# Seven products instead of eight for ten row tiles of an output projection, with four of the seven gathered in one PSUM bank

## The chip, the cores and the metric

The kernel runs on one core of one Trainium2 chip. The metric is the device time of one execution in microseconds; every operand is fp32. Matrix products in full precision are made of three passes: each operand is split into a high part and the rest (a low part), and high x high, high x low and low x high are summed in PSUM. So a product over 128 rows, 512 columns and a depth of 128 is three matmuls, here called one chunk.

The engines are TensorE (PE; PEld is its weight load), VectorE (DVE), ScalarE (ACT), GpSimd (POOL) and SyncE (SP), which issues nearly all DMAs. ACT, DVE, POOL, SP and PE all run their instructions in the order in which the program writes them (`manual_schedule`); a wait at the head of one of them holds up all that stands behind it there.

## The reference

An encoder layer of two halves, for 256 prompt and 2048 sample rows (2304 together, T in the code, 18 tiles of 128 rows):

```python
q, k, v, z_a, u_f, z_f = jnp.split(rms_norm(x, g_pre) @ w_in, ...)
y_a = neighbourhood_attention(q, k, v, rpb)
y_f = fourier_mix(u_f, w_fourier, b_fourier)
mixed = concatenate([rms_norm(y_a, g_na) * silu(z_a),
                     rms_norm(y_f, g_f) * silu(z_f)], -1)
return x + rms_norm(mixed @ w_out, g_post)
```

`mixed @ w_out` has a depth of 1024: 512 of the attention half, 512 of the Fourier half, and 1024 output columns. The row scale of each half's norm is applied to the half's product, as it comes out of PSUM; g_na and g_f are folded into the weights.

## The kernel before

The program first makes all projections and the Fourier half (to about 598 us). Then comes the attention phase: 36 groups G[k], k = 0 to 35 (4 pairs of heads, pr, times 9 blocks of queries, i), one per step of the loop at L1642, and at last 18 tiles of the attention half's output product (L1804).

A step k does on PE, in this order: `scores` of group k (into four PSUM banks: three of tag `a`, which has three, one of tag `b`, which has two); the first transposes of group k-1 (`transp`, into the two banks `ptb`); half of an output product of the Fourier half (`f_mm`, 6 matmuls, L1497); the second transposes of k-1; the other half (6 matmuls); `pv` of k-1 (into the one bank of tag `c`). The Fourier half's output product is here to fill PE: step k makes output half n = k % 2 of row tile k // 2, a depth of four chunks, into one bank of tag `b` (`po`). `f_evac` takes it out with the row scale `invf`: DVE for n = 0 (L1529), ACT for n = 1 (L1526), which also stores the 128 x 1024 row tile to `oD`.

On the other engines in a step: `bias_max` (four on DVE, L1251) and `exps` (four on ACT) of group k; `soft`, two calls of two scalings each, on POOL (L1263); the copies of the transposes (h = 0 on ACT, L1572, h = 1 on DVE, L1574); `split_q` of group k+1 (qh on ACT, ql on POOL, L1209); every second step `ys_split` of the next row tile (yh on ACT, L1483, yl on DVE, L1488) and `ys_mul` (the product with silu(z) on POOL, L1474); in steps with i = 5 to 8 `split_k` for the next pair of heads (kh on ACT, L1140, kl on POOL, L1141); then y (DVE, L1600) and its square (ACT L1606, POOL L1607) from `pv`. `norm_sums` and `norm_turn` make the row scales at the steps of the table NT.

Tiles come from pools with a fixed number of buffers; a new tile of a tag waits until the oldest one of that tag has been read for the last time. `gt` takes from a pool of 13 buffers of 4 KB a partition (output tiles `ofs`, the Fourier weights `wo1`: eight tiles `wo1[n][c]` of output half n and chunk c, high and low part).

Of the kernel before, what the change touches and what calls it, by code (L numbers as in the profile page):

```python
# [10 lines left out]
F32 = mybir.dt.float32  # L11
F32R = mybir.dt.float32r
AF = mybir.ActivationFunctionType
ALU = mybir.AluOpType
# [160 lines left out]
def build(tc, A, O):  # L175
# [1262 lines left out]
    gpb = sm.tile([128, D], F32, name="gpb", bufs=1)  # L1438
# [24 lines left out]
    def ys_load(d):  # L1463
# [4 lines left out]
        if half:  # L1468
            d["z"] = sm.tile([128, 4, 128], F32, tag="yz", name="yz", bufs=1)
            nc.sync.dma_start(d["z"], zD[0, :, ts].rearrange("(c p) t -> p c t", p=128))  # L1470
# [5 lines left out]
    def y_parts(d):  # L1476
        d["h"] = sm.tile([128, 4, 128], F32R, tag="yh", name="yh", bufs=3)
        d["l"] = sm.tile([128, 4, 128], F32R, tag="yl", name="yl")
# [6 lines left out]
    def y_lo(d):  # L1485
        if "l" not in d:
            d["l"] = sm.tile([128, 4, 128], F32R, tag="yl", name="yl")
        V.tensor_tensor(out=d["l"], in0=d["raw"], in1=d["h"].bitcast(F32), op=ALU.subtract)  # L1488
# [14 lines left out]
    def xt_load(d):  # L1503
        d["xt"] = gt([128, D], F32, "xt")
        nc.sync.dma_start(d["xt"], A["xn"][d["t"] * 128:d["t"] * 128 + 128, :])
# [7 lines left out]
    def a_mm(d, n, js=range(12)):  # L1513
        if js[0] == 0:
            d["p", n] = ps.tile([128, 512], F32, tag="a" if n else "b", name="po", bufs=3 if n else 2)
        out_mm(d, n, js, d["p", n], lambda n, x, c: WO[x][:, c, n * 512:n * 512 + 512])
# [62 lines left out]
    def pv(g):  # L1579
# [28 lines left out]
        if R is None or hc:  # L1608
            nc.sync.dma_start(yD[0, pr, :, ts], y)

    WO = []

    WK = (24, 26, 28, 29, 31, 32, 33, 34)
    NT = {4: range(2, 4), 8: range(4, 8), 10: range(8, 12), 11: range(12, 16), 12: range(16, 18),
          32: range(4), 34: range(4, 8), 36: range(8, 12)}

# [25 lines left out]
    for k in range(2, len(G) + 1):  # L1642
# [13 lines left out]
        if k == 9:  # L1656
            nc.sync.dma_start(gpb, pbc(A["gpost"]))
        if k == 23:
            wp = pt.enter_context(tc.tile_pool(name="wp", bufs=1, side="right"))
            WO.extend(wp.tile([128, 4, D], F32R, name="w0%d" % x) for x in range(2))  # L1660
        if k in WK:
            y = WK.index(k)
            nc.sync.dma_start(WO[y % 2][:, y // 2].bitcast(F32), woD[y % 2, y // 2])
        x = k // 2 + 1
        if g:
            scores(g)
            if 2 < k < 34 and k % 2 == 0:
                ys_mul(ftiles[x])
                if x + 1 < 18:
                    ys_load(ftiles[x + 1])  # L1670
            bias_max(g, 0, 0)
            exps(g, 0, 0)
            bias_max(g, 0, 1)
            bias_max(g, 1, 0)
# [3 lines left out]
        if g:  # L1678
            exps(g, 0, 1)
            bias_max(g, 1, 1)  # L1680
            exps(g, 1, 0)
            f_mm(k, range(6))
# [21 lines left out]
        if g:  # L1704
            f_mm(k, range(6, 12))
        else:
            a_mm(atiles[0], 1, range(6))
        if k % 2 and x < 18:
# [5 lines left out]
        if g:  # L1714
            f_evac(k)
# [6 lines left out]
        if k == 12:  # L1722
            pq_.close()
        if k + 1 < len(G):
            prep_v(G[k + 1])
        if k + 3 < len(G):
            prep(G[k + 3])
        if k == 28:
            xk = [kp.tile([128, T], F32, tag=x, name="xk") for x in ("kh", "kl")]
        if 32 <= k < 36:  # L1730
            x, d = k - 32, atiles[k - 32]
            d["xt"] = xk[x // 2][:, x % 2 * D:x % 2 * D + D]
            nc.sync.dma_start(d["xt"], A["xn"][d["t"] * 128:d["t"] * 128 + 128, :])
        if k == 32:
            ys_load(atiles[0])
        if k in (34, 35):
            ys_load(atiles[k - 33])
            of_load(atiles[k - 34])


    def evac(d, p, ns, q):
# [3 lines left out]
        jk = sm.tile([128, 512], F32, tag="jk", name="jk", bufs=1)  # L1745
# [36 lines left out]
    def last_tile(d, b):  # L1782
        og = d["og"] = gt([128, D], F32, "og")
        nc.gpsimd.tensor_tensor(out=og[:, :512], in0=d["of"][:, :512], in1=gpb[:, :512], op=ALU.mult)
        for q, ns in enumerate((slice(512, 896), slice(896, 1024))):
            p = ps.tile([128, 384], F32, tag="a", name="pl", bufs=3)[:, :ns.stop - ns.start]
            for j in range(12):
                c, x = divmod(j, 3)
                nc.tensor.matmul(p, (d["l"] if x == 2 else d["h"])[:, c], WO[x == 1][:, c, ns], start=j == 0,
                                 stop=j == 11)  # L1790
# [13 lines left out]
    for j, d in enumerate(atiles):  # L1804
        if j + 3 < 18:
            ys_load(atiles[j + 3])
        for x in range(2, 5) if j == 0 else (j + 4,):
            if x < 18:
                of_load(atiles[x])
                if x > 3:  # L1810
                    xt_load(atiles[x])
# [40 lines left out]
```

## Time and profile before

| | |
|---|---|
| median of 3 runs | 958.79 us (958.73 to 958.92) |
| span of the profiled execution | 957.4 us (its own time is not listed) |
| mean granted TensorE clock | 0.997 |
| PE busy | 949.5 us, 5625 matmuls |
| DVE, ACT, POOL busy | 707.8, 494.8, 435.4 us |
| attention phase with the Fourier half's product | about 598 to 847 us |
| steps k = 12, 13, 14, 15, 16 begin | 677.3, 684.7, 692.2, 699.7, 707.1 us |

A row of a timeline reads: start, duration (us), engine, line, operation, output <- inputs, shapes, how many; in brackets the idle time of the engine just before and what ended it. A row of a source line reads: how many, and the shortest, median and longest duration in ns. A row by stretch reads: the stretch, its length, then busy time and count of PE, PEld, DVE, ACT, POOL, then the granted clock, the DMA share and GB/s. Durations of neighbours on DVE and ACT overlap by some 0.07 us.

### The profile page before, as it was taken

To read this page: it belongs to the slowest core of one execution; us is meant where nothing else is said; L and a number is where in the kernel's file an instruction comes from. 1 tells how busy PE (TensorE), PEld (TensorE's weight loads), DVE (VectorE), ACT (ScalarE), POOL (GpSimd) and SP (SyncE) were. 2 spreads that over 40 slices of the span, in tenths; PEclk is the share of its full clock that TensorE was granted. 3 is DMA by queue.
4 is the path that set the end of the run, shared out by engine and by line. 5 is a ranking of instruction groups with operands and counts; after the bars stand their busy time and mean duration, and the time that the engine had idled before them with its cause. 6 is when DMAs were issued, how large, how long until landed. Compare 5 with 4: busy or idle time off the path is not lost.

```text
span 957.4 us, 16751 instructions
## 1 busy us (share of the span) xinstructions
PE 949.5 (99%) x5625; PEld 790.3 (83%) x5625; DVE 707.8 (74%) x1298; ACT 494.8 (52%) x1068; POOL 435.4 (45%) x411
## 2 busy tenths in 40 slices
PE   9999999999999999999999999999999999999997
PEld 8889988888888888888888779788788888888886
DVE  6758987787975865697887369776666656659997
ACT  6735676423334532233344267677676766644443
POOL 4100002465750302575566055567678686524444
PEclk9999999999999999999999999999999999999998
DMA  9899697557758894499889997788877998989993
GB/s 357 297 383 334 245 343 264 187 193 280 296 190 331 304 342 144 175 345 356 306 297 340 335 329 247 232 241 271 262 241 239 285 301 255 287 289 346 330 346 129
DMA packets 140077, 269.80 MB, mean 282 GB/s; under 512 B 13178, under 2 KB 80464, under 8 KB 136728
## 3 DMA queue, kind: packets, MB, share of 16 engines
q1 hardware_dynamic: 139640, 268.32, 80.5%
q8 instruction: 45, 0.74, 0.3%
q10 hardware_dynamic: 288, 0.40, 0.1%
q14 instruction: 40, 0.33, 0.1%
q0 software_dynamic: 64, 0.02, 0.0%
HBM read 179.00 MB, written 96.81 MB: 288 GB/s over the span
## 4 chain that ended last, share of the span: by engine, by line
PE 98%; DVE 1%; DMA 0%; issue 0%; DVEq 0%
PE po L1497 20%; PE mm L166 18%; PE mm L164 18%; PE mm L165 18%; PE pv L1586 6%; PE ptb L1570 6%; PE s L1229 4%; PE py L164 1%; PE py L165 1%; PE py L166 1%; PE ptb L1043 1%; DMA x<-x 0%; PE pab L1053 0%; PE ppq L1096 0%; PE pz L166 0%; PE pz L164 0%
## 5 line engine op out<-in xcount | busy, mean ns | idle before, releaser
L164 PE MATMUL mm<-xh,wa 128*128 128x512 f32 x448 | 174.4, 389 | 0.0
L165 PE MATMUL mm<-xl,wa 128*128 128x512 f32 x448 | 174.3, 389 | 0.0
L166 PE MATMUL mm<-xh,wa 128*128 128x512 f32 x448 | 174.3, 389 | 0.0
L545 POOL TENSOR_TENSOR ws<-wr 128x512 f32<-128x512 f32 x16 | 23.4, 1465 | 217.8 <-DVE wa L560 127.6
L1263 POOL TENSOR_SCALAR w<-w,m 128x465 f32<-128x465 f32 (+9 forms) x136 | 84.8, 635 | 46.2 <-DVE m L1260 35.5
L166 PEld LDWEIGHTS mm<-xh,wa 128*128 128x128 f32 x448 | 84.1, 188 | 17.6
L164 PEld LDWEIGHTS mm<-xh,wa 128*128 128x128 f32 x448 | 84.1, 188 | 17.5
L165 PEld LDWEIGHTS mm<-xl,wa 128*128 128x128 f32 x448 | 84.1, 188 | 17.4
L1497 PE MATMUL po<-wo,yh 128*128 128x512 f32 x272 | 90.5, 414 | 0.0
L560 DVE TENSOR_TENSOR wa<-wr,wa 128x512 fp32r<-128x512 f32 x60 | 71.8, 1205 | 22.0 <-ACT wa L559 21.8
L1497 PE MATMUL po<-w,yh 128*128 128x512 f32 x280 | 86.8, 391 | 0.0
L1256 ACT ACTIVATE w<-w,m 128x465 f32<-128x465 f32 (+9 forms) x136 | 78.3, 579 | 13.7 <-DVE m L1251 13.3
L1251 DVE CUSTOM_DVE_ANT_1 w<-s,tb 128x465 f32<-128x465 f32 (+8 forms) x124 | 61.2, 531 | 10.1 <-PE s L1229 9.6
L165 PE MATMUL mm<-vl,xh 128*128 128x512 f32 x168 | 65.5, 390 | 0.0
L598 POOL TENSOR_TENSOR mt<-mt,rmask 128x880 f32<-128x880 f32 (+2 forms) x24 | 50.8, 2129 | 32.2 <-DVE mt L594 20.1
L164 PE MATMUL mm<-vh,xh 128*128 128x512 f32 x168 | 65.4, 389 | 0.0
L166 PE MATMUL mm<-vh,xl 128*128 128x512 f32 x168 | 65.4, 389 | 0.0
L1574 DVE COPY pt<-ptb 120x384 f32<-120x384 f32 (+5 forms) x72 | 40.5, 562 | 28.6 <-PE ptb L1570 27.8
L891 DVE TENSOR_TENSOR f<-u,mm 128x512 f32<-128x512 f32 x64 | 43.4, 679 | 24.2 <-PE mm L166 19.7
L1497 PEld LDWEIGHTS po<-w,yh 128*128 128x128 f32 x280 | 52.2, 188 | 10.9 <-issue 0.4
L1570 PE MATMUL ptb<-ident,w 128*120 128x128 f32 (+8 forms) x422 | 58.8, 276 | 0.0
L1586 PEld LDWEIGHTS pv<-pt,v 120*64 120x64 f32 (+9 forms) x880 | 47.4, 136 | 12.9 <-issue 9.7
(287 smaller groups left out, 2369.8 us busy)
## 6 DMA issues: line engine op xcount, KB each, us to landing
wr<-wz SPq DMA_DIRECT2D x48, 512.0 KB
vl<-sD SPq DMA_DIRECT2D x20, 512.0 KB
xm<-xm SPq DMA_DIRECT2D x9, 1024.0 KB
oD<-ofs SPq DMA_DIRECT2D x18, 512.0 KB
of<-oD SPq DMA_DIRECT2D x18, 512.0 KB
yr<-yD SPq DMA_DIRECT2D x34, 256.0 KB
zD<-f SPq DMA_DIRECT2D x16, 512.0 KB
xD<-nx SPq DMA_DIRECT2D x14, 512.0 KB
```

The source lines that it names most:

```text
L164: nc.tensor.matmul(out, lh, rh, start=first, stop=False)
L165: nc.tensor.matmul(out, lh, rl, start=False, stop=False)
L166: nc.tensor.matmul(out, ll, rh, start=False, stop=last)
L560: nc.vector.tensor_tensor(out=o[:, 1], in0=src, in1=o[:, 0].bitcast(F32), op=ALU.subtract)
L598: nc.gpsimd.tensor_tensor(out=o, in0=i, in1=rmask[:, m0:m0 + n].unsqueeze(2).to_broadcast([128, n, 80]), op=ALU.add)
L891: nc.vector.tensor_tensor(out=dst(f, b), in0=src(uu[u]), in1=src(p), op=op)
L1251: nc.vector.tensor_tensor_reduce(out=rows(g["w"][b][:, h, :n], w), in0=rows(g["s"][2 * b + h][:, :nr * sw(w)], sw(w))[:, :, :w], in1=tv, s ...
L1256: nc.scalar.activation(w, w, AF.Exp, bias=m[:, h:h + 1], scale=-1.0, accum_out=m[:, 2 + h:3 + h])
L1263: nc.gpsimd.tensor_scalar(w, w, m[:, 4 + h:5 + h], 1.0, ALU.mult, ALU.mult)
L1497: nc.tensor.matmul(p, (d["l"] if x == 2 else d["h"])[:, c], w(n, int(x == 1), c), start=j == 0, stop=j == 11)
L1570: nc.tensor.transpose(ptb[h][:nk, j * 128:j * 128 + 128], g["w"][b][:, h, c0:c0 + nk], ident)
L1586: nc.tensor.matmul(p[hs, b], g["v"][:nk, v, hs], g["pt"][b][:nk, h, j * 128:j * 128 + 128], start=j == 0, stop=j == len(ch) - 1)
```

## The change

Row tiles 8 to 17 go in five pairs, a pair to four steps (k = 16 to 35; s = 0 to 3 is the step in its pair). With A the two row tiles (a, b) cut into depth halves, and B the weights cut into depth halves and output halves, the eight quarter products become seven (Strassen's scheme in Winograd's form), each two chunks deep, 6 matmuls. Sums of the weights, T1 = B12 - B11, T3 = B22 - B12, T2 = B22 - T1, T4 = B21 - T2, are made once; those of the rows, S1 = b1 + b2, S2 = S1 - a1, S3 = a1 - b1, S4 = a2 - S2, in each pair.

X is one PSUM bank of tag `b` that is held for the pair's four steps: P = a1 B11 at s = 0, then S2 T2, S3 T3 and b2 T4 are added to what is there at s = 1, 2, 3; in between it is read out each time (`p_evac`). Z is a bank of tag `a`: a2 B21, S1 T1 and S4 B22 at s = 0, 1, 2, and nothing at s = 3. In a step, X's product stands where the first half of `f_mm` stood, Z's where the second stood. Seven evacuations a pair go to ACT (copies with scale) and to DVE (scaled additions onto the output tile in SBUF).

```diff
+    def t_load(j):
+        for x in range(2):
+            TR[j, x] = qt([128, D], F32, "wt")
+            nc.sync.dma_start(TR[j, x], A["wo"][1, j + 2 * x])
+    def t_scale(j):
+        for x in range(2):
+            c = 4 + j + 2 * x
+            nc.scalar.activation(TR[j, x], TR[j, x], AF.Copy, scale=gmix[:, c:c + 1])
+    def t_sums(j):
+        a1, a2, b1, b2 = [TR[j, x][:, n * 512:n * 512 + 512] for x in range(2) for n in range(2)]
+        for e, o, i0, i1 in ((nc.gpsimd, a1, a2, a1), (V, a2, b2, a2), (nc.gpsimd, b2, b2, a1), (V, b1, b1, b2)):
+            e.tensor_tensor(out=o, in0=i0, in1=i1, op=ALU.subtract)
+    def t_split(j, x, low):
+        src = TR.pop((j, x)).rearrange("p (n e) -> p n e", n=2)
+        h, l = TT[j, x] = qt([128, 2, 512], F32R, "th"), low([128, 2, 512], F32R, "tl")
+        nc.scalar.copy(h, src)
+        V.tensor_tensor(out=l, in0=src, in1=f_(h), op=ALU.subtract)
+    TS = {11: ((t_load, 0),), 12: ((t_scale, 0), (t_sums, 0), (t_load, 1)), 13: ((t_split, 0, 1, qt),),
+          14: ((t_split, 0, 0, qt), (t_scale, 1)), 15: ((t_sums, 1), (t_split, 1, 1, gt)), 16: ((t_split, 1, 0, gt),)}
...
+    def p_sums(P):
...
+            nc.gpsimd.tensor_tensor(out=o, in0=i0, in1=i1, op=op)
+    def p_split(P, s):
+        if s == -1:
+            ys_split(P["d"][0])
+        if s == 0:
+            part_split(P, "S21", P["S"][:, :4], 4)
+        if s == 1:
+            part_split(P, "S3", P["d"][1]["raw"], 4)
+            part_split(P, "S4", P["S"][:, 4:], 2)
...
+        if n == 0:
+            if s < 2:
+                copy(o0[:, hi if s else lo], s0)
+            elif s == 2:
+                add(o1[:, hi], s1)
+            else:
+                copy(o1[:, lo], s1)
+                store(o1, t1)
+        elif s < 3:
+            add(o0[:, hi if s else lo], s0)
+            if s == 1:
+                o1 = P["o"][1] = gt([128, D], F32, "ofs")
+                copy(o1[:, hi], s1)
...
+        pairs(k, p_evac, 0, 3, 0)
         if g:
...
+        for t, *a in TS.get(k, ()):
+            t(*a)
+        if g and k < P0:
             f_mm(k, range(6, 12))
+        elif g:
+            pairs(k, p_mm, 0, 3, 1)
...
+        pairs(k, p_evac, 0, 2, 1)
+        pairs(k, p_split, -1, 1)
         if pr < 3 and i in (5, 6, 7, 8):
             split_k(KK[pr + 1], i - 5)
-        if g:
+        if k < P0:
             f_evac(k)
```

`p_sums` stands on POOL at s = 0 ahead of the step's `soft`; S21 holds S2 and S1 side by side. A new pool of seven 4 KB buffers (`qt`) holds the weight sums, later a part of the attention half's weights and the residual tiles `xt`; it opens after k = 10, for which the row scales of NT move one step earlier (steps 9, 10, 11). The attention half's weights, one tile of 8 blocks before, now lie in the buffers of the key tiles, in `qt` and in `gt`. Four `xt` tiles were loaded at k = 32 to 35; now two at k = 35 and three at the start of the final phase. `gpb` is loaded at k = 34, not 9.

How the instructions stand, at three places. DVE at the end of step 12 and the start of step 13, before (ofs is the evacuation of step 12's po, y that of pv, the rows of w,m are bias_max):

```order
L1260 RECIPROCAL m<-m 128x2
L1448 TENSOR_TENSOR dt<-dy 128x2
L1449 TENSOR_TENSOR dt<-dt,ds 128x2
L1450 SCALAR_TENSOR_TENSOR invf<-dt,dy 128x2
L1529 TENSOR_SCALAR ofs<-po,invf 128x512
L1600 TENSOR_TENSOR y<-pv,za 128x2x8x16
L1251 ISA w,m<-s,tb 128x465
```

and now (wt is a weight tile being summed):

```order
L1577 COPY pt<-ptb 88x384
L1260 RECIPROCAL m<-m 128x2
L1638 TENSOR_TENSOR wt<-wt 128x512 x2
L1532 TENSOR_SCALAR ofs<-po,invf 128x512
L1603 TENSOR_TENSOR y<-pv,za 128x2x8x16
L1251 ISA w,m<-s,tb 128x465
```

The row scales' three short operations went to step 11, and two links of the chain of sums came in ahead of ofs. DVE at the end of step 15 and the start of step 16, before:

```order
L1574 COPY pt<-ptb 120x512
L1260 RECIPROCAL m<-m 128x2
L1488 TENSOR_TENSOR yl<-yr,yh 128x512
L1600 TENSOR_TENSOR y<-pv,za 128x2x8x16
L1251 ISA w,m<-s,tb 128x276
```

and now (tl is the low part of a weight tile):

```order
L1577 COPY pt<-ptb 120x512
L1260 RECIPROCAL m<-m 128x2
L1638 TENSOR_TENSOR wt<-wt 128x512 x2
L1644 TENSOR_TENSOR tl<-wt,th 128x1024
L1491 TENSOR_TENSOR yl<-yr,yh 128x512
L1603 TENSOR_TENSOR y<-pv,za 128x2x8x16
L1251 ISA w,m<-s,tb 128x276
```

Two links and a split of 1024 columns came in ahead of the row tile's own low part. On ACT the high part of the same weight tile stands between qh and yh of step 15, and so ahead of kh and of the evacuation of po. PE in step 19, the last of the first pair, from the first output product to pv, before:

```order
L1497 MATMUL po<-wo_5086,yh 128x512 x2
L1497 MATMUL po<-wo_5086,yl 128x512
L1497 MATMUL po<-wo_5087,yh 128x512 x2
L1497 MATMUL po<-wo_5087,yl 128x512
L1570 MATMUL ptb<-ident,w 80x128 x4
L1497 MATMUL po<-wo_5088,yh 128x512 x2
L1497 MATMUL po<-wo_5088,yl 128x512
L1497 MATMUL po<-wo_5089,yh 128x512 x2
L1497 MATMUL po<-wo_5089,yl 128x512
L1586 MATMUL pv<-pt,v 64x128 x8
```

and now:

```order
L1660 MATMUL px<-th,yh 128x512
L1660 MATMUL px<-tl,yh 128x512
L1660 MATMUL px<-th,yl 128x512
L1660 MATMUL px<-th,yh 128x512
L1660 MATMUL px<-tl,yh 128x512
L1660 MATMUL px<-th,yl 128x512
L1573 MATMUL ptb<-ident,w 80x128 x4
L1589 MATMUL pv<-pt,v 64x128 x8
```

Six matmuls are gone, and pv follows the second transposes at once.

More of the change, by code (lines that the diff above doesn't have):

```diff
@@ new lines, in B_, with product @@
+    def B_(name):
+        n, x = {"11": (0, 0), "21": (0, 2), "22": (1, 2)}.get(name, (None, None))
+        if n is not None:
+            return [(wo1[n][x + c][:, 0], wo1[n][x + c][:, 1]) for c in range(2)]
+        x, n = {"T1": (0, 0), "T3": (0, 1), "T4": (1, 0), "T2": (1, 1)}[name]
+        return [(TT[c, x][0][:, n], TT[c, x][1][:, n]) for c in range(2)]
+    def product(p, a, name, first):
+        h, l = a
+        for c, (bh, bl) in enumerate(B_(name)):
+            for i, (y, b) in enumerate(((h, bh), (h, bl), (l, bh))):
+                nc.tensor.matmul(p, y[:, c], b, start=first and c == i == 0, stop=c == 1 and i == 2,
+                                 skip_group_check=not first)
@@ new lines, in p_mm @@
+    def p_mm(P, s, n):
+        if n == 0:
+            if s == 0:
+                P["X"] = ps.tile([128, 512], F32, tag="b", name="px", bufs=2)
+            a = half_of([P["d"][0][x] for x in "hl"], 0) if s == 0 else half_of(P[("S21", "S3", "S3")[s - 1]], s == 3)
+            product(P["X"], a, ("11", "T2", "T3", "T4")[s], s == 0)
+        elif s < 3:
+            P["Z"] = ps.tile([128, 512], F32, tag="a", name="pz", bufs=3)
+            a = (half_of([P["d"][0][x] for x in "hl"], 1), P["S21"] and half_of(P["S21"], 1), P["S4"])[s]
+            product(P["Z"], a, ("21", "T1", "22")[s], True)
@@ L1681, in build @@
             exps(g, 1, 0)
-            f_mm(k, range(6))
+            if k < P0:
+                f_mm(k, range(6))
+            pairs(k, p_mm, 0, 3, 0)
             soft(g, 0)
```

120 lines of the change are left out of this document (87 added, 33 removed).

## The prediction

> **What bounds the kernel now.** I read the page first: the busy shares, then the chain that ended last.
>
> ```profile
> PE 949.5 (99%) x5625; PEld 790.3 (83%) x5625; DVE 707.8 (74%) x1298; ACT 494.8 (52%) x1068; POOL 435.4 (45%) x411
> ...
> PE 98%; DVE 1%; DMA 0%; issue 0%; DVEq 0%
> ```
>
> PE is busy from end to end and is the chain. So each matmul taken out is worth its spacing, and each microsecond that PE is made to wait is lost whole, because PE has no slack to swallow it. What decides is whether the other engines can still feed it. So I went to the timeline of PE for one attention step (k=13) and the start of the next, then k=15 and 16:
>
> ```profile
> 684.68 0.49 PE L1229 MATMUL s<-kh,qh 64*128 64x480 f32 x2
> ...
> 686.04 0.87 PE L1570 MATMUL ptb<-ident,w 128*120 128x128 f32 x6
> 686.66 0.71 PE L1497 MATMUL po<-wo,yh 128*128 128x512 f32 x2
> ...
> 688.13 1.03 PE L1570 MATMUL ptb<-ident,w 128*120 128x128 f32 x8
> 688.92 0.70 PE L1497 MATMUL po<-wo,yh 128*128 128x512 f32 x2
> ...
> 690.49 1.75 PE L1586 MATMUL pv<-pt,v 120*64 120x128 f32 x28
> 692.17 0.43 PE L1229 MATMUL s<-kh,qh 64*128 64x360 f32 x2
> ...
> 709.11 0.71 PE L1497 MATMUL po<-wo,yh 128*128 128x512 f32 x2
> ...
> 710.58 0.82 PE L1570 MATMUL ptb<-ident,w 128*120 128x128 f32 x6
> ```
>
> A step is 7.49 us: scores, transposes, half an output product (6 matmuls), transposes, the other half (688.92 to 690.49: 1.57 us), pv. The same stretch on the engines that feed it:
>
> ```profile
> 683.42 0.74 DVE L1529 TENSOR_SCALAR ofs<-po,invf 128x512 f32<-128x512 f32 x1
> ...
> 684.80 0.42 DVE L1600 TENSOR_TENSOR y<-pv,za 128x256 f32<-128x256 f32 x1 [0.64 <-PE pv L1586]
> 685.65 0.64 DVE L1251 CUSTOM_DVE_ANT_1 w<-s,tb 128x465 f32<-128x465 f32 x1 [0.42 <-PE s L1229]
> ...
> 687.23 0.55 DVE L1574 COPY pt<-ptb 120x384 f32<-120x384 f32 x1
> ...
> 689.21 0.69 DVE L1574 COPY pt<-ptb 120x512 f32<-120x512 f32 x1 [0.86 <-PE ptb L1570]
> ```
>
> ```profile
> 682.75 0.73 POOL L1209 TENSOR_TENSOR ql<-ql,qh 128x256 fp32r<-128x256 f32 x1 [0.68 <-ACT qh L1208]
> 683.46 1.29 POOL L1263 TENSOR_SCALAR w<-w,m 128x465 f32<-128x465 f32 x2
> ```
>
> ```profile
> 705.85 1.54 POOL L1263 TENSOR_SCALAR w<-w,m 128x360 f32<-128x360 f32 x2
> 707.36 1.42 POOL L1141 TENSOR_TENSOR kl<-kl,kh 128x576 fp32r<-128x576 f32 x1
> ```
>
> The reader is to see how late Pool is: its second softmax scaling ends (684.75) when PE is already at the next step's scores (684.68), while DVE evacuates the output product (ofs, 683.42) well before that.
>
> **The change part by part.** Seven products of 6 matmuls replace eight halves in each of 5 pairs: one half, 1.57 us, goes at each pair's last step: 5 x 1.57 = 7.85 us. There, pv stands directly behind the second transposes and loses the cover for their copies. In k=13 that copy runs to 689.90; without the half, pv would begin at 688.92 and want it for its second half, 0.87 us on, at 689.79: 0.1 us each. Term 1: 0.5 - 7.85 = **-7.35**.
>
> *The sums of the weights.* At k=12 and k=15 t_sums puts four 128x512 operations in a chain: Pool, DVE, Pool, DVE. Each DVE link waits for a Pool link, and Pool's first stands behind its second softmax scaling. DVE takes its instructions in order, so the evacuation ofs, then y, then the next bias_max stand behind the chain. The prices, from lines of this trace with the nearest shapes:
>
> ```profile
> L1474 POOL TENSOR_TENSOR yr<-yr,yz x16: 1276/1292/1303, 613.2 to 818.5; 128x512 f32<-128x512 f32 x16
> ```
>
> ```profile
> L1488 DVE TENSOR_TENSOR yl<-yr,yh x34: 678/818/1741, 619.4 to 940.5; 128x512 fp32r<-128x512 f32 x34
> ```
>
> ```profile
> L723 ACT ACTIVATE wo<-wr,gmix x4: 1144/1150/1157, 328.3 to 350.9; 128x1024 fp32r<-128x1024 f32 x4
> ```
>
> So a Pool link is 1.3 us (1.29), a DVE link 0.7 (0.68 undisturbed), a whole weight tile on ScalarE 1.15.
>
> At k=12: Pool's first sum 684.75 to 686.05, DVE to 686.75, Pool to 688.05, DVE to 688.75, ofs (0.74) to 689.5. Only two PSUM banks carry tag b: the score tile takes one, po(12) holds the other. So PE, at 686.66, waits for po(13) until 689.5: 2.85 us. Then y 0.4, and the DVE copy of the next transposes comes 1.58 after its step's first bias_max (687.23 - 685.65): 689.9 + 1.58 = 691.5. The second transposes of k=13 wait for it and for ScalarE's copy, to 691.6 where they stood at 688.13. Term 2: **+3.5** (2.85 if only the bank counts; 4.2 if the second weight tile's scaling is late).
>
> At k=15 the chain is longer, because t_split follows before the evacuation, which is ScalarE's for an odd step:
>
> ```profile
> 704.65 0.41 ACT L1208 CAST qh<-ql 128x256 fp32r<-128x256 f32 x1
> 704.95 0.62 ACT L1483 CAST yh<-yr 128x512 fp32r<-128x512 f32 x1
> 705.48 0.67 ACT L1140 CAST kh<-kl 128x576 fp32r<-128x576 f32 x1
> 706.05 0.69 ACT L1526 ACTIVATE ofs<-po,invf 128x512 f32<-128x512 f32 x1
> ```
>
> Pool's scaling ends at 707.4, kl (707.36 now) moves behind the sums. Links: 708.7, 709.4, 710.7, 711.4. ScalarE's high half of the weight tile waits for the last: 712.55; then yh, kh and ofs, 0.5 to 0.7 each: 714.4. X, the pair's first product, needs the bank of that ofs; PE is there at 709.11 and waits 5.3 us. DVE's low half (1.28, the row of L724 below) and yl end at 714.6, y at 715.0; only then come the three bias_max and the copy, 716.7. The second transposes, at 710.58 before, start at 716.5: **+5.9** in all (5.1 to 6.5).
>
> ```profile
> L724 DVE SCALAR_TENSOR_TENSOR wo<-wr,gmix,wo x4: 1277/1280/1285, 330.2 to 356.2; 128x1024 fp32r<-128x1024 f32 x4
> L1743 DVE SCALAR_TENSOR_TENSOR of<-po,inva,of x35: 736/741/752, 854.8 to 947.2; 128x512 f32<-128x512 f32 x35
> ```
>
> At k=16 the last weight tile's high half is ahead of S21's on ScalarE, and its low half (1.28) is ahead of the evacuation of Z (0.74) on DVE; Z holds one of the three banks of tag a, of which the next scores need all three. By the same addition Z is free about 1.4 us late, and 0.2 more goes at the next copy: **+1.6** (0 to 2). Terms 2 to 4 together are 11.0.
>
> *The clock.* What a wait of 5 us does to the matmuls behind it shows only at the end, after PE's last matmul, and at the start (in the two rows by stretch the last three columns are granted clock, DMA share and GB/s):
>
> ```profile
> 950.25 0.28 PE L1789 MATMUL pl<-w,yl 128*128 128x128 f32 x1
> ```
>
> ```profile
> 952.00:952.50 0.50, 0.00 (x0) 0.00 (x0) 0.39 (x3) 0.01 (x1) 0.10 (x1) 0.99 0.86 324
> 952.50:953.00 0.50, 0.00 (x0) 0.00 (x0) 0.38 (x3) 0.00 (x0) 0.00 (x0) 0.50 0.08 29
> ```
>
> ```profile
> 0.99 4.63 PE L237 MATMUL idle<-onesq 128*128 128x128 f32 x20 [0.99 <-POOL onesq L233]
> 5.68 0.80 PE L170 MATMUL mm<-wc,xh 128*128 128x512 f32 x1
> ...
> 7.08 0.39 PE L170 MATMUL mm<-wc,xh 128*128 128x512 f32 x1
> ```
>
> Two microseconds after PE stops, the granted clock falls from 0.99 to 0.50. After a cold start the first large matmul, at 5.68, still takes 0.80 against 0.39 later. If a stall lets the clock fall and it takes 3 us of work to come back, half of them is lost: 1.5; nearly 5 us cold would make it 2.4. Term 5: **+1.5** for the k=15 stall (0 to 2.4) and nothing for k=12, whose stretch of idleness is interrupted. The row's 2.0 us would put the k=12 wait at risk too: 1.5 more, kept for a rival. The trace shows no stall in the middle.
>
> The Trainium skill ("TensorE: Matmul & The Clock Gate", section "What's actually happening") has a free-running window of about 3.4 us, idle for the fall and busy for the rise. By the page alone the k=12 wait is safe, the k=15 wait need not fill a window, and the sum could be 1.5 lower; the row, whose clock fell after 2.0 us, is nearer to a fall, and no run here shows which.
>
> *Each pair's own work.* Four evacuations become seven, four of them DVE additions at 0.74; the halves to split grow from 1024 to 1792 columns; p_sums adds four Pool operations of 256 columns (0.73 each by the ql row). By busy time there is room: DVE 74%, ScalarE 52%, Pool 45%. In order there is less. (a) At a pair's last step ScalarE copies X (0.6) ahead of qh, so Pool's ql comes 0.6 later, and with the step 1.5 shorter the next scores ask for it about 0.35 too early. (b) At its second step DVE waits for S3's and S4's high halves, so the next bias_max is some 0.75 late and the transposes wait 0.2 to 0.3. Together 0.55 for four pairs: **+2.2** (0 to 3.5). (c) At k=24 p_sums (2.9) meets split_k (1.42) of k=23 on Pool, so ql(25) is late: **+1.0** (0 to 1.5). DMA: 2 MB of weights at k=11 and 12, and two of the final phase's xt tiles later; I cost both at nothing, as they are loaded a step or more ahead (up to 1 us if not).
>
> Sum: -7.35 + 3.5 + 5.9 + 1.6 + 1.5 + 2.2 + 1.0 = +8.35, on the profiled span of 957.4: 965.75. The profiled execution's own time is not listed; its span is 1.4 below the median of the runs, 958.79, which I keep: **967 us**.
>
> **The rivals.** *The sums don't hold PE (faster).* If Pool's first link were done before its softmax scaling, or DVE reached ofs first, the chain would lie under work that is there anyway. The place is ofs at k=12: it decides whether the chain ends by 685.9, so that ofs frees the bank by 686.66. For it: DVE is idle from 684.16 to 684.80 or thereabouts at that place, and the sums' data are loaded a step before. Against: the order of both queues. Terms 2 to 5 gone and half the pairs' work: -7.35 + 1.6 = -5.75, so 953. Chance 0.10.
>
> *Only the sums cost.* The pairs' own work hides, and the clock holds: -7.35 + 11.0 = +3.65, so 962.5. For it: the busy shares. Against: (a) and (b), which are a matter of tenths. Chance 0.22.
>
> *The clock falls twice and the pairs cost their upper bound.* -7.35 + 11.0 + 4.8 + 5.0 = +13.45: 972. For it: the 2.0 us of the row; against it, the stalls are broken by short work. Chance 0.14.
>
> *The product does not shrink.* If X's reads in between held back its next product, the half saved would be lost in waits. X ends two thirds of a step before its next product and is read at once, so no: chance 0.02, 966 to 970, and with the forecast in the time.
>
> **How the numbers follow.** Forecast (965 to 970) 0.48 with that last one's 0.02, the clock twice 0.14, only the sums 0.22; the faster rival 0.10; 0.06 for halves of the sums' stalls, which end within 0.2% of before. A measurement of this kernel can tell about 0.2% (1.9 us) from no change. Of the faster case's 0.10, 0.09 is beyond 0.2%. So faster 0.09, same 0.06, slower 0.85. The range is 960 to 973: the low end is the stalls at their least with nothing else (-7.35 + 2.85 + 5.1 = +0.6, 959.4, rounded into the slower side), the high end the clock twice with 1 us of DMA.
>
> **What would show it.** In the changed profile: PE's idle before the first L1500 matmul of k=13 about 2.9 us, released by DVE ofs; before the first px matmul about 5.3, released by ScalarE ofs; DVE waits at t_sums on Pool, four times, some 7 us in total; the granted clock below 1 just after the px stall; px and pz 210 matmuls where po had 240. I am wrong if those two waits are under 1 us, if Pool's sums stand ahead of the softmax in time, or if the time is under 957.

## The result, and the profile after

| | before | after |
|---|---|---|
| median | 958.82 us (958.73 to 958.92, 4 runs) | 987.78 us (986.15 to 989.51, 4 runs) |
| ratio, 95% interval | 1 | 1.0299 [1.0284, 1.0314] |
| span of the profiled execution | 957.4 us | 984.0 us (its time 986.15) |
| matmuls; mean granted clock | 5625; 0.997 | 5595; 0.990 |

The change is slower, as forecast, but by 29 us and not by 8: the time lies outside the range. The page of after shows thirty matmuls fewer, yet PE's busy time is not less but 3.9 us more (949.5 before). In part that is because some matmuls ran at half the clock: the steps k = 16 and 32, where it fell, hold 4.6 us more of busy time. The rest, up to 0.5 us in each of the other steps and 2.7 us in the final phase, was not traced:

```profile
PE 953.4 (97%) x5595; PEld 786.4 (80%) x5595; DVE 715.2 (73%) x1326; ACT 512.6 (52%) x1096; POOL 454.9 (46%) x435
```

PE bounds the kernel, so the place where a step's `scores` begin on PE is a ruler: the delay of each step against the same step of before, read from the two timelines of PE, gives a price for each step. This is the whole difference of the spans, beside what the prediction put there:

| stretch | after - before, us | predicted |
|---|---|---|
| up to k = 12, and the origin of time | -0.3 | 0 |
| k = 13 (weight sums of k = 12) | +3.6 | +3.5 (Term 2) |
| k = 14, 15, 16 (weight sums of k = 15, the clock) | +7.7 | +7.4 (Terms 3 and 5) |
| k = 17 (Z late) | +1.2 | +1.6 (Term 4) |
| last step of each pair (k = 19, 23, 27, 31, 35) | -5.9 | -7.35 (Term 1) |
| other steps of the pairs, without k = 17 and 32 | +8.3 | +3.2 (a, b, c) |
| k = 32 | +6.1 | no term of its own |
| final phase: 4.1 up to PE's last matmul, 1.9 behind it | +6.0 | 0 (up to 1) |
| sum | +26.6 | +8.35 |

The two stalls that the prediction described are there, in the timeline of PE of after, with their sizes (2.85 and 5.3 forecast):

```profile
689.16 0.72 PE L1500 MATMUL po<-wo,yh 128*128 128x512 f32 x2 [2.54 <-DVE ofs L1532]
...
718.40 1.22 PE L1660 MATMUL px<-wo,yh 128*128 128x512 f32 x2 [5.32 <-ACT ofs L1529]
719.41 0.63 PE L1660 MATMUL px<-wo,yl 128*128 128x512 f32 x1
719.84 1.05 PE L1660 MATMUL px<-wo,yh 128*128 128x512 f32 x2
720.69 0.63 PE L1660 MATMUL px<-wo,yl 128*128 128x512 f32 x1
721.12 1.18 PE L1573 MATMUL ptb<-ident,w 128*120 128x128 f32 x6
...
836.04 0.67 PE L1229 MATMUL s<-kh,ql 64*128 64x360 f32 x2 [3.48 <-POOL ql L1209]
```

The reader is to see two things. The six px after the long stall take 2.72 us (718.40 to 721.12) where six cost 1.47 in the last step of the last pair (863.26 to 864.73), so the clock fell. And there is a third stall, at k = 32, of which the prediction knew nothing. The rows by stretch (granted clock third from the end) show the half clock around both:

```profile
715.10:718.40 3.30, 0.00 (x1) 0.01 (x1) 2.13 (x3) 2.72 (x4) 0.56 (x1) 0.50 0.00 0
718.40:721.80 3.40, 3.40 (x10) 2.71 (x11) 2.79 (x12) 2.91 (x9) 3.32 (x4) 0.50 0.68 221
721.90:725.30 3.40, 3.40 (x38) 2.70 (x36) 1.54 (x3) 3.39 (x8) 3.40 (x7) 1.00 0.90 262
...
836.00:841.30 5.30, 5.26 (x20) 4.22 (x21) 2.94 (x10) 2.62 (x8) 4.55 (x7) 0.50 0.95 291
```

*Where the third stall comes from.* On POOL, `ys_mul` of the pair's second tile stands at k = 31 ahead of the softmax and of ql, and waits 5.6 us for its z tile:

```profile
826.41 0.73 POOL L1610 TENSOR_TENSOR ysq<-ysq,sqa 128x256 f32<-128x256 f32 x1 [0.28 <-ACT sqa L1609]
832.77 1.26 POOL L1477 TENSOR_TENSOR yr<-yr,yz 128x512 f32<-128x512 f32 x1 [5.63 <-DMA yz<-zD]
834.01 1.29 POOL L1263 TENSOR_SCALAR w<-w,m 128x465 f32<-128x465 f32 x2
835.26 0.72 POOL L1209 TENSOR_TENSOR ql<-ql,qh 128x256 fp32r<-128x256 f32 x1
```

SP's queue tells why. There is one buffer for z tiles, so the second tile's load has to stand behind the multiplication of the first (POOL, 821.17 to 822.44, in step k = 30). There a table of 960 KB and a weight tile of 512 KB are ahead of it in the queue; it goes out at 825.2, 2.7 us after that multiplication ended, and its own multiplication starts 7.6 us later:

```profile
823.57 0.33 SPq L1154 DMA_DIRECT2D tb<-tD  x1
824.54 0.37 SPq L1804 DMA_DIRECT2D wk<-woD  x1
825.19 0.37 SPq L1473 DMA_DIRECT2D yz<-zD  x1
```

*The final phase.* There SP's queue repeats the same order as before (store, yr, of, xt). What changed is the pool that the xt tiles come from: before, the first four lay in the old key tiles and the rest came from the 13 buffers; now all come from the pool of 7, one of which holds a weight tile to the end. SP's timeline, one tile of it:

```profile
942.85 0.33 SPq L1508 DMA_DIRECT2D xt<-xn  x1
943.27 0.86 SPq L1928 DMA_DIRECT2D yo<-xt  x2
944.23 0.46 SPq L1466 DMA_DIRECT2D yr<-yD  x1
944.73 1.10 SPq L1504 DMA_DIRECT2D of<-oD  x1
949.50 0.33 SPq L1508 DMA_DIRECT2D xt<-xn  x1
```

The xt load of 949.50 has to wait until the store of 943.27, the last one ahead of it, has landed; the next stores stand behind the load, and the yr load behind them. So a tile takes what a store takes to land and a little more, 5.4 to 7.0 us from one xt load to the next (6.2 in the mean of nine, 893.36 to 949.50), and no longer PE's 5.4. The waits of SP and of ScalarE, us in total, times and longest:

```profile
SPq L1508 <- DMA yo<-xt: 38.3, 14, 5.0
...
ACT yh L1486 <- DMA yr<-yD: 33.5, 12, 3.8
```

The list of before has no row for either.

### The profile page after: what moved, and what is told of

The parts are those of the page before. It is cut to its first block, busy times and chain, and to the rows that moved or that the text cites. A ratio compares the mean times of both kernels' runs of the same rounds, so it can differ in the third digit from the quotient of the medians.

```text
span 984.0 us, 16772 instructions
## 1 busy us (share of the span) xinstructions
PE 953.4 (97%) x5595; PEld 786.4 (80%) x5595; DVE 715.2 (73%) x1326; ACT 512.6 (52%) x1096; POOL 454.9 (46%) x435
## 5 line engine op out<-in xcount | busy, mean ns | idle before, releaser
L1500 PE MATMUL po<-wk,yh 128*128 128x512 f32 x280 | 87.4, 393 | 1.4 <-ACT yh L1486 1.2
L1927 POOL TENSOR_TENSOR xt<-of,xt 128x512 f32<-128x512 f32 x34 | 43.2, 1291 | 56.8 <-issue 35.2
L1500 PEld LDWEIGHTS po<-wk,yh 128*128 128x128 f32 x280 | 51.8, 188 | 13.6 <-ACT yh L1486 3.2
L1573 PEld LDWEIGHTS ptb<-ident,w 128*120 128x120 f32 (+8 forms) x422 | 48.1, 143 | 17.4 <-issue 8.0
L559 ACT CAST wa<-wr 128x512 fp32r<-128x512 f32 x60 | 36.5, 618 | 43.1 <-PE mm L166 19.6
```

Source lines behind the costliest of these rows:

```text
L1500: nc.tensor.matmul(p, (d["l"] if x == 2 else d["h"])[:, c], w(n, int(x == 1), c), start=j == 0, stop=j == 11)
L1573: nc.tensor.transpose(ptb[h][:nk, j * 128:j * 128 + 128], g["w"][b][:, h, c0:c0 + nk], ident)
L1927: nc.gpsimd.tensor_tensor(out=xt[:, ns], in0=of[:, ns], in1=xt[:, ns], op=ALU.add)
```

## The experiments

All against the kernel after (987.78) and, on the same chip, the kernel before. The step prices are read as above.

### The final phase: one tile less in flight (e1)

```diff
             if x < 18:
                 of_load(atiles[x])
-                xt_load(atiles[x])
+            if 2 < x < 19:
+                xt_load(atiles[x - 1])
```

> Against the changed kernel (987.8): the final phase alone is touched, each xt tile is loaded one tile later. Theory: the store of a tile and the next xt load chase each other through six slots on SP's queue (load waits for the store just issued, 5 to 6 us), and the yr loads behind it come late; with a tile less in flight the 6.0 us that the final phase lost come back: 982 (981 to 983). Rival, the transfers' bytes bound it (1 MB more in that phase): no change, 987 to 988.

Measured: 981.18 us (980.17 to 983.81), ratio 1.0237 [1.0222, 1.0252]. PE's delay no longer grows in the final phase (0.0 instead of 4.1), and the tail behind PE's last matmul is 7.5 us (6.9 before, 8.7 after). SP now shows store, yr, of, xt without a gap ahead of xt, at a pitch of 5.42 us:

```profile
918.02 1.59 SPq L1928 DMA_DIRECT2D yo<-xt  x2
919.70 0.51 SPq L1466 DMA_DIRECT2D yr<-yD  x1
920.27 0.77 SPq L1504 DMA_DIRECT2D of<-oD  x1
921.09 0.48 SPq L1508 DMA_DIRECT2D xt<-xn  x1
923.44 1.58 SPq L1928 DMA_DIRECT2D yo<-xt  x2
```

The same bytes go over, so the rival (bytes) falls, and the loop of store and load is shown.

### The weight sums on one engine (e2)

```diff
-((nc.gpsimd, a1, a2, a1), (V, a2, b2, a2), (nc.gpsimd, b2, b2, a1), (V, b1, b1, b2))
+((V, a1, a2, a1), (V, a2, b2, a2), (V, b2, b2, a1), (V, b1, b1, b2))
```

> Against the changed kernel (987.8): all four differences of the weight tiles on VectorE, none on Pool. Theory: VectorE, in order, waits for Pool's links, and the bank and the next softmax wait behind it; without those waits the k=12 step loses some 1.5 instead of 3.6 us, the k=15 and k=16 steps some 2 to 3 instead of 7.6, with no fall of the clock: 980 (978.5 to 982). Rival, the scaling of the weight tiles and their split on ScalarE hold the chain: 985 or more.

Measured: 981.38 us (980.65 to 985.99), ratio 1.0245 [1.0221, 1.0268]. k = 13 costs 1.9 instead of 3.6, k = 15 1.8 instead of 0.4, k = 16 4.6 instead of 7.2. PE's stalls are now 0.9 and 2.4 where they were 2.5 and 5.3:

```profile
687.37 0.73 PE L1500 MATMUL po<-wo,yh 128*128 128x512 f32 x2 [0.92 <-DVE ofs L1532]
...
715.18 0.74 PE L1660 MATMUL px<-wo,yh 128*128 128x512 f32 x2 [2.37 <-ACT ofs L1529]
```

VectorE's waits for POOL are real, but of the 12.4 us of steps 13 to 17 only 3.1 go with them in the profiled run (9.4 are left); in that run the final phase also cost 2.1 instead of 4.1, so part of the gain in the median isn't theirs (the edit does not touch that phase). But the clock did fall, which the theory did not expect: the stall of 2.37 us was enough.

### z a step earlier (e3), z with two buffers (e6)

```diff
         if s == -3:
             ys_load(d1, False)
-        if s == -2:
             ys_mul(d0)
             z_load(d1)
```

> Against the changed kernel (987.8): the first tile of a pair is multiplied one step earlier, so the z tile of the second is loaded a step earlier. Theory: the 6.1 us of the k=32 step come from Pool standing 5.6 us at the multiplication for a z tile that was queued behind a 0.96 MB table and 1.5 MB of others; gain 4 to 5.5: 983 (982 to 984). Rival, p_sums on Pool alone makes ql late there as in the other pairs and the z wait hides: 987 or more.

Measured: 984.5 us (981.1 to 987.84; two runs near 981.5, two near 987.5), ratio 1.0255 [1.0225, 1.0286]. The k = 32 step costs 0.0, but in the profiled run (987.84) k = 30 costs 7.0: POOL now waits for the first tile's z.

```profile
820.11 1.27 POOL L1477 TENSOR_TENSOR yr<-yr,yz 128x512 f32<-128x512 f32 x1 [4.59 <-DMA yz<-zD]
```

The wait had moved, so the edit was the wrong cure. The right one gives z a second buffer and more distance:

```diff
-        d["z"] = sm.tile([128, 4, 128], F32, tag="yz", name="yz", bufs=1)
+        d["z"] = sm.tile([128, 4, 128], F32, tag="yz", name="yz", bufs=2)
...
         if s == -4:
             ys_load(d0)
+            z_load(d1)
...
             ys_mul(d0)
-            z_load(d1)
```

> Against the changed kernel (987.8): two buffers for the z tiles, both loaded at the pair's start, four steps ahead, the multiplications where they were. Theory: the single buffer made the z load late; in the run that multiplied the first tile a step earlier the wait only moved to the first tile's z (4.6 us at k=30), so nothing stands against it; now no z wait on Pool is over 1 us, the k=32 step loses 0.5 to 1.5 instead of 6.1, and the clock does not fall there: 983 (982 to 984). Rival, Pool is late at k=32 by its own work: 986 or more.

Measured: 978.22 us (977.49 to 979.13), ratio 1.0202 [1.0184, 1.0219]. The k = 32 step costs 0.0, the granted clock stays at 1.00 from 820 to 840, and POOL's two multiplications of that pair stand without a wait:

```profile
821.09 1.27 POOL L1477 TENSOR_TENSOR yr<-yr,yz 128x512 f32<-128x512 f32 x1
...
827.01 1.30 POOL L1477 TENSOR_TENSOR yr<-yr,yz 128x512 f32<-128x512 f32 x1
```

The gain, 9.6, is more than the 5 expected: 6.2 at k = 32, where I had thought that POOL's own work would keep 0.5 to 1.5, and 2.0 in the final phase, up to PE's last matmul. That second part need not be the z buffer's: the final phase costs 2.1 here, but also 2.1 in e2 and 2.0 in e9, which do not touch it either, and SP's waits for the xt buffers are still 37.2 us. So 6.1 us hung on one buffer of 2 KB a partition and on the place of its load; the run changes both, and the place needs the buffer.

### POOL's work in a pair (e4, e5)

```diff
-        if s == 0:
-            p_sums(P)
...
             soft(g, 1)
+            pairs(k, lambda P, s: p_sums(P), -1, -1)
```

> Against the changed kernel (987.8): the four sums of a pair are made on Pool at the end of the step before the pair's first one instead of ahead of the softmax of its first one. Theory: they (2.9 us) make ql of the pair's second step late, about 0.5 to 1.7 us in each of four pairs; gain 2 to 4: 985 (984 to 986). Rival, the evacuations on VectorE and ScalarE cost those steps their time: no change, 987 to 988.

Measured: 989.53 us (987.68 to 991.87), ratio 1.0321 [1.0301, 1.0341]. The waits for ql are the same to 0.01 us (0.68 at k = 21, 1.52 at k = 25), so the theory seemed to fall. But POOL was busy without a gap there: the sums passed one instruction of 0.73 us and stayed ahead of ql. The run says nothing on the theory. What it lost is in part that at k = 15 the sums came ahead of those of the weights (the px stall at k = 16 became 7.9 us), and in part the clock: it fell at k = 13 and at k = 25, whose stalls (2.54 and 1.52 us) are those of the kernel after, and these steps cost 4.7 and 3.4 instead of 3.6 and 1.8. e5 is the same edit with the sums on VectorE:

```diff
-            nc.gpsimd.tensor_tensor(out=o, in0=i0, in1=i1, op=op)
+            V.tensor_tensor(out=o, in0=i0, in1=i1, op=op)
```

> Against the changed kernel (987.8): the four sums of a pair on VectorE, which idles at the end of the step before the pair, and none on Pool. In the run that only moved them on Pool they passed one instruction of 0.73 us and stayed ahead of the next ql, so it told nothing. Theory: on Pool they make ql late at a pair's second step (PE waits 0.69 at k=21 and 1.52 at k=25); both go and the steps after them start earlier: 985.5 (984.5 to 986.5). Rival, the evacuations set those steps: 987 or more.

Measured: 987.3 us (985.65 to 988.01), ratio 1.0291 [1.0276, 1.0307]: no gain within the scatter. The steps say why. What ql had cost is gone (k = 21 from 0.9 to 0.0, k = 25 from 1.8 to 0.0), and most of it is back one step earlier (k = 20 from 0.5 to 0.8, k = 24 from 0.15 to 1.3, k = 28 from 1.7 to 4.9, with a z wait of 1.2 on POOL and a fall of the clock in it), where VectorE has four more operations ahead of the next step's `bias_max` (that this is the way back was argued from the order, not tried). The pairs of k = 20 and 24 come out 0.6 better each. The mechanism (c) of the prediction is right, but its removal costs nearly as much elsewhere.

### The weight sums spread over the steps (e7, e9), all cures together (e8, e10)

At most one difference of 128x512 on each of the two engines in a step; VectorE never waits for a link that POOL makes in the same step. e9's table:

```diff
-    TS = {11: ((t_load, 0),), 12: ((t_scale, 0), (t_sums, 0), (t_load, 1)), 13: ((t_split, 0, 1, qt),),
...
+    TS = {11: ((t_load, 0), (t_load, 1)),
+          12: ((t_scale, 0, 0), (t_scale, 0, 1), (t_link, 0, 0, V), (t_link, 0, 1, U)),
+          13: ((t_link, 0, 2, V), (t_link, 0, 3, U), (t_scale, 1, 0), (t_scale, 1, 1)),
+          14: ((t_split, 0, 0, W), (t_link, 1, 0, V), (t_link, 1, 1, U)),
+          15: ((t_link, 1, 2, V), (t_split, 0, 1, W), (t_link, 1, 3, U)),
+          16: ((t_split, 1, 0, W), (t_split, 1, 1, W1)), 17: ((t_split, 1, 1, W0),)}
```

e7 had `t_load` of the second two tiles at k = 12 and their scaling at k = 13 and 14, and its T3 of the second chunk (in e8 too) is formed from a block already overwritten, which changes values but no instruction's size.

> Against the changed kernel (987.8): the same eight differences and four splits, spread over k=12 to 17, at most 2 us of VectorE in a step, and VectorE waits for no link of Pool in the step in which Pool makes it. Theory: the 12.4 us of k=12 to k=17 come from the order of the queues and not from the work; 2 to 4 are left, and the clock holds: 978.5 (977 to 981). Rival, the work itself (8 differences, 4 splits, 4 scalings) has no room: 983 or more.

Measured: 987.14 us (981.55 to 989.57), ratio 1.0284 [1.0251, 1.0317]. k = 13 costs 0.0, but k = 14 costs 6.5: the scaling on ScalarE, ahead of the evacuation there, waited 6.0 us (5.9 in e8) for a tile that was loaded only one step before. k = 17 costs another 6.5, with a wait of 3.5 for ql. e8 had the same stall at k = 14:

> The changed kernel with the later xt tile, the sums of the pairs on VectorE, two z buffers, the spread weight sums, and the high half of q ahead of the copy of X on ScalarE. Theory: the causes are separate, so the gains add: 987.8 less 6.6, 2, 5 and 9, and 1 for the order on ScalarE: 964 (961 to 967), still over the kernel before. Rival, the waits overlap or the clock falls elsewhere: 970 or more.

Measured: 977.25 us (976.63 to 980.54), ratio 1.0196 [1.0178, 1.0214]: the gains do not add; its steps 14 to 18 cost 16.0. With all four tiles loaded at k = 11:

> Against the changed kernel (987.8): the weight sums spread over k=12 to 17 as in the run before, with one fault of that run mended: there ScalarE stood 5.9 us at a scaling for a weight tile loaded one step earlier, so it measured another wait; now all four tiles are loaded at k=11. Theory: the 12.4 us are an order of queues, at most 2 us of VectorE work now stand in a step: 2.5 to 4 us are left, the clock holds: 978.5 (977 to 981). Rival, the work has no room there: 983 or more.

Measured: 986.79 us (981.81 to 988.36), ratio 1.0284 [1.0255, 1.0313]; the profiled run took 981.81. Steps 13 to 17 cost 0.0, 0.8, 2.5, 1.2 and 4.95: 9.5 instead of 12.4, and the clock fell at k = 17. So this order of the queues does not free the 8 to 10 us that the theory gave to it; in the orders tried, five steps have no room for this work. The new waits are for `ofs` (1.2) and for ql (1.0 and 3.2); POOL, which makes two of its four links from 702 to 724, has no gap there:

```profile
703.97 0.73 PE L1500 MATMUL po<-wo,yh 128*128 128x512 f32 x2 [1.18 <-DVE ofs L1532]
...
711.69 0.41 PE L1229 MATMUL s<-kh,ql 64*128 64x288 f32 x2 [0.97 <-POOL ql L1209]
...
722.48 0.69 PE L1229 MATMUL s<-kh,ql 64*128 64x384 f32 x2 [3.17 <-POOL ql L1209]
```

e10 has e9's table, e1's and e6's cures, qh ahead of the copy of X on ScalarE, and the second multiplication and the four sums of a pair on VectorE, two of them in the step before the pair and two in its first:

```diff
+        if s:
+            V.tensor_tensor(out=b, in0=b, in1=P["d"][1]["z"], op=ALU.mult)
...
+        for o, i0, i1, op in ops[:2] if s else ops[2:]:
+            V.tensor_tensor(out=o, in0=i0, in1=i1, op=op)
```

> The changed kernel with all the cures: later xt tile, two z buffers, spread weight sums, high half of q ahead of the copy of X, and the second multiplication and the four sums of a pair on VectorE, two in the step before the pair and two in its first. Theory: 987.8 less 9 (weight sums), 9.6 (z, measured with what it freed in the final phase), 4.6 (the rest of the final phase) and 2 to 3 (Pool): 962 (959 to 965). Rival, each pair costs on VectorE what it saves on Pool: 965 to 968.

Measured: 976.3 us (975.33 to 978.19), ratio 1.018 [1.0163, 1.0197]: far from the 962 expected. The final phase and k = 32 are cured (0.0 and 0.6), but steps 14 to 18 cost 17.2 in the profiled run. The granted clock fell after the waits of 3.5 us at k = 14 and 2.7 us at k = 17. The first of them nobody had thought of:

```profile
701.80 0.95 PE L1589 MATMUL pv<-pt,v 120*64 120x128 f32 x13 [3.51 <-DMA v<-vD]
```

The v tiles of the attention are late. The kernel before has no such wait, and e10 to e13 have it (0.6 to 3.5 us), all with weight tiles loaded at k = 11 or 12; but e9 has e10's weight loads and no such wait, and no run leaves the loads out, so this cause is argued and not shown.

### Four pairs, and nine steps for the weight sums (e11)

As e10, with `P0 = 20`, at most two differences or one split in a step, k = 12 to 20, all on VectorE.

> The same with four pairs instead of five (tiles 10 to 17) and the weight sums spread over k=12 to 20, at most 1.4 us of VectorE in a step and nothing of them on Pool. Theory: the weight sums cost under 1.5 us, the four pairs gain 1.0 to 1.4 each at their last step and lose 0.5 to 1.5 each before: 958.5 (956.5 to 961), level with the kernel before. Rival, the pairs lose more than the half is worth wherever they stand: 962 or more.

Measured: 967.36 us (966.36 to 968.24), ratio 1.009 [1.0075, 1.0105]. The steps up to k = 19, where the weight sums stand, still cost 3.4, the first pair 3.9 more than before (3.45 of it at k = 21, where a split and the evacuation of Z share VectorE); the other three pairs come out at -0.3, +0.8 and +1.1. The best version found with the weight sums in it is still slower than before. The rival holds in its time, and in its reason but for one pair: that of k = 24 gains 0.3.

### What the pairs cost without the weight sums (e12, e13)

The four weight tiles are loaded, but nothing is made of them; the products take plain weights, so the output of tiles 8 to 17 is not the reference's.

```diff
-    TS = {11: ((t_load, 0),), 12: ((t_scale, 0), (t_sums, 0), (t_load, 1)), 13: ((t_split, 0, 1, qt),),
...
+    TS = {11: ((t_load, 0),), 12: ((t_load, 1),)}
...
-        n, x = {"11": (0, 0), "21": (0, 2), "22": (1, 2)}.get(name, (None, None))
+        n, x = {"11": (0, 0), "21": (0, 2), "22": (1, 2), "T1": (0, 0), "T3": (0, 2), "T4": (1, 0), "T2": (1, 1)}[name]
```

> Against the changed kernel (987.8): the four weight tiles are loaded but neither scaled, summed nor split, and the products that need the sums take the plain tiles instead, so the output of tiles 8 to 17 is not the reference's; PE's work is the same. Theory: the weight sums with what stands behind them cost 12.4 with the fall of the clock at k=16 (steps k=13, 15, 16 and 17 by the two traces); without them 975.4 (974 to 977), the z wait and the final phase left as they are. Rival, the pairs' own evacuations hold those steps: 980 or more.

Measured: 978.7 us (976.16 to 980.91), ratio 1.0207 [1.0189, 1.0226]: a gain of 9.1 where 12.4 was expected, between the theory and the rival. Steps 13 to 17 still cost 5.2 (0.0, 1.6, 0.4, 2.4, 0.8): v is late (a wait of 1.5), and ql is late at k = 16 (2.1). In the kernel after, both lay under the longer stalls. So the work on the weights itself is worth 7.2 of the 12.4. At k = 20 this run loses 3.7 instead of 0.5: POOL waits 2.1 us for a z tile, PE 1.8 for ql, and the clock falls.

e13 is the same with e10's other cures:

> The same left out (so again no valid output of tiles 8 to 17), with the cures of the run with five pairs: later xt tile, two z buffers, order on ScalarE, second multiplication and sums of a pair on VectorE. It prices the pairs alone. Theory from the steps of that run: pairs of k=24, 28 and 32 come out at -0.25, +1.27 and +1.21, that of k=20 at +0.3, the first at about +0.3: 961.5 (959.5 to 963), so the pairs don't gain even for free. Rival, by the prediction's first term the halves are worth 7.35: 951.5 to 956.

Measured: 962.56 us (961.42 to 966.97, 7 runs), ratio 1.0051 [1.0034, 1.0068]. With the weight sums for nothing (but for the loads of their tiles) and every wait cured for which a cure was found, the change is still 3.8 us slower than the kernel before. In the profiled run the v wait costs 2.2 at k = 14 and the five pairs -0.7, +0.3, -0.25, +1.6 and +1.15, +2.1 in all. So the time is close to the 961.5 expected, but partly by luck: the pairs cost 0.7 less than the theory had them, and the v wait was not in it. PE's longest waits there:

```profile
PE pv L1589 <- DMA v<-vD: 1.9, 1, 1.9
PE ptb L1573 <- ACT pt L1575: 1.9, 4, 0.6
PE ptb L1573 <- ACT nsb L1549: 1.3, 2, 1.0
PE s L1229 <- POOL ql L1209: 1.0, 1, 1.0
```

That is the verdict on the idea: a half saves 1.0 to 1.4 us at the end of a pair, and the three steps before it give back 0.6 to 2.8, in waits of 0.2 to 1.0 for ScalarE and POOL.

## Why the prediction was wrong in size

*Right.* That PE is the bound, that the saved half is lost by waits for in-order queues, and which: Terms 2, 3 with 5, and 4 measured 3.6, 7.7 and 1.2 against 3.5, 7.4 and 1.6; the VectorE waits at the weight sums came to 10.3 us in four waits (some 7 forecast). Within Terms 3 and 5 the split is another one: the 0.6 that Term 3 gave to VectorE's copy behind X does not show, as that copy ended at 720.65, while the px at half the clock ran to 721.12; and 0.4 at k = 15 had no term.

*The step that failed* is the sentence "DMA: 2 MB of weights at k=11 and 12, and two of the final phase's xt tiles later; I cost both at nothing, as they are loaded a step or more ahead (up to 1 us if not)". I counted the distance in steps and not what a load has to wait for before it is issued. Two limits of buffers decided. The one z buffer was there before, with two steps from a load to its use; now the second tile of a pair has one step (6.1 at k = 32; e6 takes it away). And the xt tiles now have six buffers, where a load waits for the last store ahead of it (6.0 in the final phase; e1 takes 5.4 of it away). Together they are 12.1 of the 18.3 us that the sum was short. The change's own lines show both (`z_load` behind `ys_mul(d0)`, `xt_load` from `qt`), and SP's queue is in order like the others. The weights' load was perhaps not free either: e12 and e13 show PE waiting 1.5 to 2.0 for v, which the kernel before does not, and which would lie under a longer stall in the kernel after.

*The pairs' own work* was mis-sized: (a), (b) and (c) forecast 3.2 and measured 8.3 without k = 32. (c) is there, 1.5 us of wait at k = 25 in a step that costs 1.8; but ql is late at k = 21 too (0.7 of 0.9), where no split_k was forecast to meet the sums. (a), 0.35 at the start of the next pair, is 0.5 at k = 20 and 0.15 at k = 24. (b), 0.2 to 0.3 in a pair's third step, is 0.4 to 1.1 there, so it was sized at half or less. And k = 28 costs 1.7, for which there was no term: PE waits 1.45 for ql, as POOL has no gap from 792.8 to 808. `ys_mul`, which now comes in two consecutive steps of a pair instead of every second step, is 1.29 of that stretch; but with the second multiplication on VectorE (e13) 1.0 of the wait is still there, and a pair of POOL's scalings takes 1.83 instead of 1.23, so the cause of that step is not settled.

*Term 1* is -5.9 and not -7.35: the last steps gain 1.0, 1.4, 1.35, 1.2 and 1.0 instead of 1.47. By this difference what the missing half covered was worth 0.1 in one example, and up to 0.5 in others; PE's idle time in these steps is under 0.2, so no single wait shows it. The prediction counts seven evacuations in a pair; there are eight instructions (four on ScalarE, four on VectorE), since Z is read twice at s = 1. Its chances leave 0.01 of the faster case within 0.2% and give it to slower instead of same.

*The clock* fell twice, as one rival had it, but at k = 16 and k = 32 and not at k = 13. At k = 16 the px and the transposes behind them lost 1.6 (1.5 forecast), of which VectorE's copy behind X, named above, would have taken an estimated 0.8 in any case (at the full clock the px would end 1.47 after 718.40, at 719.87). At k = 32 some 2.6 of the 6.1 are the clock (6.1 less the 3.5 of idle time).

## What to carry to other kernels

When a kernel has one engine busy to 99%, a saving on it is worth only what its feeders leave; add up each feeder's instructions by queue and by step before believing that shares of busy time leave room. Of every load that a change moves, ask which buffer it takes, whose last use frees that buffer, and what stands behind the load in its queue: here a load one step ahead of its use, through one buffer, cost 6.1 us, as much as the five saved halves gained (5.9). After a wait is cured, measure again: in e3, e9 and e12 another wait stood in its place.

## What the runs showed of the hardware

*The clock fell for 3.4 us or twice that.* Read in steps of 0.1 us, the half clock lasts from 715.0 to 721.8 and from 834.5 to 841.3 in the kernel after (6.8 us each), and 3.45 us in e3 (690.0 to 693.5). The stall of 2.54 us at k = 13 is the same in six kernels; the clock held in after, e1, e5 and e6 and fell in e3 and e4. Shorter stalls lost it too: 1.52 us at k = 25 in e4 and 1.44 us at k = 28 in e9, where the kernel after kept it through stalls of the same size (1.52 and 1.45). The rows by stretch of e3:

```profile
686.80:690.00 3.20, 0.69 (x3) 0.60 (x4) 2.09 (x4) 0.31 (x1) 1.07 (x1) 1.00 1.01 392
690.10:693.40 3.30, 3.30 (x13) 2.57 (x12) 2.15 (x10) 3.16 (x10) 0.76 (x2) 0.50 1.08 355
693.50:696.00 2.50, 2.50 (x27) 1.96 (x28) 1.79 (x3) 2.50 (x5) 2.50 (x3) 1.00 1.03 372
```

and of after, the same place:

```profile
686.60:689.10 2.50, 0.02 (x1) 0.00 (x0) 1.34 (x3) 0.00 (x0) 1.12 (x1) 1.00 1.03 402
689.10:692.50 3.40, 2.78 (x15) 2.17 (x16) 3.02 (x13) 2.79 (x9) 0.96 (x2) 1.00 1.05 345
```

In e3 PE had been back at work for 0.7 us when the clock fell, so the fall isn't due so many microseconds after the stop: it came 2.0 us after it in both stalls of the kernel after, 3.3 in e3, and about 3.4 in e2 at k = 16. The two microseconds that the prediction took from one row are no rule. The Trainium skill ("TensorE: Matmul & The Clock Gate", section "What's actually happening") has a free-running window of about 3.4 us; the lengths of 3.45 and 6.8 agree with it, and so does a stall of 2.5 us that sometimes costs the clock and sometimes does not. If its "idle window" is to mean one without any matmul, that does not agree: the 3.4 us before the fall hold 0.9 us of matmuls in e3 and 1.4 in both falls of the kernel after.

*VectorE and POOL take longer beside each other.* The sums of a pair on VectorE took 0.42 to 0.54 at k = 27 of e5 and up to 0.95 at k = 15 of e8; a pair of POOL's softmax scalings of 128x360, which took 1.10 at other places, took 3.02 beside VectorE's sums and splits there. VectorE's and POOL's rows of e8:

```profile
710.18 0.87 DVE L1683 TENSOR_TENSOR ysum<-yr 128x256 f32<-128x256 f32 x1 [0.16 <-POOL yr L1477]
711.08 0.76 DVE L1683 TENSOR_TENSOR ysum<-ysum,yr 128x256 f32<-128x256 f32 x1
711.76 0.95 DVE L1683 TENSOR_TENSOR yr<-yr 128x256 f32<-128x256 f32 x1
```

```profile
712.41 3.02 POOL L1263 TENSOR_SCALAR w<-w,m 128x360 f32<-128x360 f32 x2
```

The Trainium skill ("SBUF — State Buffer", section "SBUF: two separate sides") says that a VectorE operation with two inputs in SBUF and a POOL operation that reads SBUF hold the shared pair of ports exclusively; these rows fit it. It was not tried apart whether this alone keeps e9 and e10 from their expected times.
